# Negated softmax sum, division on GpSimd, and gated norms of two chunks in one

## The chip, the cores and the metric

The kernel runs on one core of one Trainium2 chip. Its time is the device time of one execution in microseconds (us); three runs of the kernel before took 1565.5, 1568.16 and 1681.18 us, and the median is 1568.16 us. Engines are called by the profile's names: PE is TensorE's matmuls and PEld its weight loads, DVE is VectorE, ACT is ScalarE, POOL is GpSimd, SP is SyncE, whose queue issues most DMAs.

## What is computed

One layer over 1024 latent tokens and 256 context tokens, width 1024. Half of the width goes through a gated DeltaNet (4 heads of 128, a forward and a backward scan, summed), half through neighbourhood attention (8 heads of 64, a window of keys and all context keys). Both go through one output projection; a SwiGLU network follows. The change touches two places: the attention's softmax and the norm that closes the DeltaNet.

```
S = S * exp(g_last) + k_dec^T v_new                    # scan step, carried state
o = rms_norm(o_f + o_b, out_norm_w) * silu(z)          # gated norm, per head
s = concatenate([q k_win + bias, q k_ctx])             # per query: 384 places of the window, 256 context keys
p = softmax(s)                                         # one softmax over both
```

## The kernel before, in words

The work comes in stages, in program order: modulation and input projections; tables for the scan; then a stage in which the two scans and the attention run beside each other; then the output projection (L1282, L1432) and the network (L1305, L1646). A scheduler lays out each engine's instructions near the order in which the program issues them; after that each engine's queue is in order.

*Scan.* Tokens are cut into ten chunks of 128, two of context (0, 1) and eight latent ones (2 to 9). `ORDER` gives each direction its order: forward 0 to 9, backward 1, 0, 9 down to 2. The loop at L1246 takes ten steps, called scan steps 0 to 9 here; each issues the loads for the next (`load`, six DMAs of 256 KB a chunk) and runs one chunk of each direction. `scan(d, c)` is a generator: keys times state (L1163, corrected at L1165), queries times state (L1173, into the sum `oacc` at L1176 or L1179), the triangular product (L1182, scaled at L1186 and L1188), the local product (L1194, added at L1195), and the state's update (L1199, L1205). A latent chunk is visited twice, once by each direction; from step 6 on both chunks of a step are visited for the second time, and `scan` goes on into `finish(c)`.

*Gated norm.* `finish` loads `z`, squares `oacc` on ACT with a sum for each head (L1220), computes the reciprocal root from an integer guess and three Newton steps on DVE (`rsqrt`, L179 to L184), scales by it and by `z` (L1227), and two turns later transposes the chunk on PE and splits it in two for the output projection (`turned`, L1109, L1112, L1113). It issues 14 small DVE instructions on 128x4 numbers. The two chunks that end last are turned only behind the first matmuls of the output projection.

*Attention beside the scan.* `attention` is a generator too. It goes through 32 pairs of halves; a half is 128 queries of one head against 640 scores. Each `next` of a scan or finish generator is a turn, and each turn adds `PACE` = 0.72 steps of attention (`beside`). `pair` computes a pair's scores into PSUM (L302), and for each half adds the bias and takes the maximum (L304, in place in the bias tile `bt`), negates the maximum (L306), takes the exponential with its sum (L307, ACT), the reciprocal (L308) and the product with it (L309). Two steps later come five transposes a half (L314), a copy out of PSUM (L317), and the values' products (L324). Bias tiles come by DMA (L271), their context part by a memset on GpSimd (L270), one pair ahead, in four buffers. GpSimd's only other work here is the split of finished attention output (L372), twice a pair of heads.

Of the kernel before, what the change touches and what calls it, by code (L numbers as in the profile page):

```python
# [9 lines left out]
F32 = mybir.dt.float32  # L10
# [3 lines left out]
AF = mybir.ActivationFunctionType  # L14
OP = mybir.AluOpType
# [44 lines left out]
def run(*gens):  # L60

    live = [g for g in gens if g is not None]
    while live:
        live = [g for g in live if next(g, 0) != 0]
# [24 lines left out]
def hybrid(ctx, tc, a, dbg):  # L89
# [20 lines left out]
    bias = lasting("bias", [128, 8])  # L110
# [142 lines left out]
    def attention(nw):  # L253

        def load(hd):
            qs = nw.tile([128, L], F16, name="qs", tag="qs", bufs=4)
            kh = nw.tile([128, T], F16, name="kh", tag="kh", bufs=4)
            kl = nw.tile([128, T], F16, name="kl", tag="kl", bufs=4)
            sp.dma_start(qs, nq_d[hd].rearrange("i d t -> (i d) t"))
            for i in range(2):  # L260
                sp.dma_start(kh[i * 64:i * 64 + 64], nk_d[0, hd])
                sp.dma_start(kl[i * 64:i * 64 + 64], nk_d[1, hd])
            return qs, kh, kl

        def biases(hp, half, cb):

            out = []
            for u, w0 in enumerate(WIN):
                bt = nw.tile([128, 640], F32, name="bt", tag="bt", bufs=4)
                pool.memset(bt[:, CTX[w0]], 0.0)  # L270
                sp.dma_start(bt[:, w0:w0 + 384], a["rpb"][2 * hp + u, half, CASE[cb]])  # L271
                out.append(bt)
            return out

        def values(hp, half, cb):
            vw = nw.tile([128, 3, 128], F32, name="vw", tag="vw", bufs=3)
            sp.dma_start(vw, vw_d[:, cb, half:half + 3, hp * 128:hp * 128 + 128])
            return vw

        def context(hp):  # L280
            vc = nw.tile([128, 2, 128], F32, name="vc", tag="vc")
            sp.dma_start(vc, nv_d[0:CT, hp * 128:hp * 128 + 128].rearrange("(c p) d -> p c d", p=128))
            return vc

        def pair(heads, bts, vw, vc, half, cb, out):

            r0 = 4 * half
            sc = psum[-1].tile([128, 1536], F32, name="sc", tag="sc", bufs=2)
            mx = nw.tile([128, 2, 4], F32, name="mx", tag="mx", bufs=3)
            for u, (head, w0, bt) in enumerate(zip(heads, WIN, bts)):  # L290
                qs, kh, kl = head
                q = qs[:, (half * 4 + cb) * 128:(half * 4 + cb + 1) * 128]
                kv = [kx[:, CT:].rearrange("p (r c) -> p r c", c=64)[:, r0:r0 + 12, BLKS[cb]:BLKS[cb] + 32]
                      for kx in (kh, kl)]
                parts = [(CTX[w0].start, CTX[w0].stop, (kh[:, 0:CT], kl[:, 0:CT]))]
                if w0:
                    parts += [(256, 512, [x[:, 0:8] for x in kv]), (512, 640, [x[:, 8:12] for x in kv])]
                else:
                    parts += [(0, 384, kv)]
                for n0, n1, ks in parts:  # L300
                    for i in range(2):
                        pe.matmul(sc[:, u * 640 + n0:u * 640 + n1], q, ks[i], start=i == 0, stop=i == 1)  # L302
                m = mx[:, u]
                dve.tensor_tensor_reduce(bt, sc[:, u * 640:u * 640 + 640], bt, 1.0, -3.0e38, OP.add, OP.max,  # L304
                                         m[:, 0:1])
                dve.tensor_scalar(m[:, 1:2], m[:, 0:1], -1.0, None, op0=OP.mult)  # L306
                act.activation(bt, bt, AF.Exp, bias=m[:, 1:2], accum_out=m[:, 2:3])  # L307
                dve.reciprocal(m[:, 3:4], m[:, 2:3])  # L308
                dve.tensor_scalar(bt, bt, m[:, 3:4], None, op0=OP.mult)  # L309
            yield 1  # L310
            pts = []
            for u, bt in enumerate(bts):
                for j in range(5):
                    pe.transpose(sc[:, u * 640 + j * 128:u * 640 + (j + 1) * 128],  # L314
                                 bt[:, j * 128:(j + 1) * 128], ident)
                pt = nw.tile([128, 640], F32, name="pt", tag="pt", bufs=3)
                act.copy(pt, sc[:, u * 640:u * 640 + 640])  # L317
                pts.append(pt)
            yield 1
            for j in range(5):  # L320
                for u, (w0, pt) in enumerate(zip(WIN, pts)):
                    vals = [vc[:, i] for i in range(2)] + [vw[:, i] for i in range(3)]
                    vv = (vals[j] if w0 else vals[(j + 2) % 5])[:, u * ND:u * ND + ND]
                    pe.matmul(sc[u * ND:u * ND + ND, 1280:1408], vv, pt[:, j * 128:(j + 1) * 128],  # L324
                              start=j == 0, stop=j == 4)
            act.copy(out.rearrange("p (r b c) -> p r b c", r=8, b=4)[:, :, cb],
                     sc[:, 1280:1408].rearrange("p (r c) -> p r c", r=8))
            yield 1

        order = [(hp, half, cb) for hp in range(NAH // 2) for half in range(2) for cb in range(4)]  # L330
        heads = {0: [load(0), load(1)]}
        vcs = {0: context(0)}
        bt, vw = biases(*order[0]), values(*order[0])
        yield 1
        old = None
        for n, (hp, half, cb) in enumerate(order):
            if half == 1 and cb in (0, 2) and hp + 1 < NAH // 2:
                heads.setdefault(hp + 1, []).append(load(2 * hp + 2 + cb // 2))
                if cb == 0:
                    vcs[hp + 1] = context(hp + 1)  # L340
            if cb == 0:
                out = nw.tile([128, 512], F32, name="no", tag="no")
            if old:
                next(old)
            cur = pair(heads[hp], bt, vw, vcs[hp], half, cb, out)
            next(cur)
            if n + 1 < len(order):
                bt, vw = biases(*order[n + 1]), values(*order[n + 1])
            yield 1
            if old:  # L350
                next(old)
                if cb == 0:
                    store(*done)
            if cb == 3:
                done = out, hp, half
            old = cur
            yield 1
        next(old)
        yield 1
        next(old)  # L360
        store(*done)
# [753 lines left out]
    with ExitStack() as gs:  # L1115
# [10 lines left out]
        def work(name, bufs=2, dt=F32):  # L1126
            return sw.tile([128, 4, 128], dt, name=name, tag=name, bufs=bufs)
# [25 lines left out]
        def scan(d, c):  # L1153
# [52 lines left out]
                                                 op0=OP.mult, op1=OP.add)  # L1206
                S[d] = sn
            yield 1
            if lat:
                if c in seen:  # L1210
                    yield from finish(c)
                seen.add(c)

        def finish(c):
            o = oacc[:, c - 2]
            z, sq = work("z"), work("sq", 1)
            sp.dma_start(fl(z), z_d[(c - 2) * 128:(c - 1) * 128])
            r = sw.tile([128, 4], F32, name="orr", tag="orr")
            for h in range(4):
                act.activation(sq[:, h], o[:, h], AF.Square, accum_out=r[:, h:h + 1])  # L1220
            t = sw.tile([128, 3, 4], F32, name="nwt", tag="nwt")
            dve.tensor_tensor(r, r, RQ2[:, c - 2], OP.mult)
            dve.tensor_scalar(t[:, 0], r, 1.0 / DH, EPS, op0=OP.mult, op1=OP.add)
            rsqrt(r, t[:, 0], t[:, 1])
            dve.tensor_tensor(r, r, RQ[:, c - 2], OP.mult)
            for h in range(4):
                dve.scalar_tensor_tensor(o[:, h], o[:, h], r[:, h:h + 1], z[:, h], op0=OP.mult, op1=OP.mult)  # L1227
            if c in last:
                return
            yield 1  # L1230
            yield 1
            turned(c)
            yield 1

        last = [ORDER[0][-1], ORDER[1][-1]]
        count = [0.0]

        def beside(n):
            count[0] += n
# [6 lines left out]
        for i in range(NCH):  # L1246
            if i + 1 < NCH:
                for d in range(2):
                    load(d, ORDER[d][i + 1])
            live = [scan(d, ORDER[d][i]) for d in range(2)]  # L1250
            while live:
                nxt = []
                for n, g in enumerate(live):
                    if next(g, 0):
                        nxt.append(g)
                    beside(PACE)
                live = nxt
        for _ in fill:
            pass

# [467 lines left out]
```

## Time and profile before

| What | Value |
|---|---|
| median of three runs | 1568.16 us |
| profiled execution | 1568.91 us, span 1566.9 us |
| busy in the span | PE 1480.1, PEld 1234.1, DVE 997.3, ACT 720.3, POOL 233.3 us |
| scan steps 2 to 5 | 619.7 to 710.4 us |
| scan steps 6 to 9 | 710.4 to 833.2 us |
| first matmul of the output projection | 833.27 us |

The page gives busy time, the span in 40 slices, the chain of work that ended last, and the costliest groups of instructions. A group's row has the line, engine and operation, output and inputs, shape and count, then busy time and mean time of one, then the engine's idle time ahead of it and what ended that. Stretches of the span can be asked for one by one; their rows give busy time and number of instructions of each engine, the granted clock as a share, the DMA engines' busy share and GB/s. Timeline rows begin with start and duration in us. Matmul records are pipelined and overlap, so a busy PE is not a full one.

### The profile page before, as it was taken

To read this page: it belongs to the slowest core of one execution; us is meant where nothing else is said; L and a number is where in the kernel's file an instruction comes from. 1 tells how busy PE (TensorE), PEld (TensorE's weight loads), DVE (VectorE), ACT (ScalarE), POOL (GpSimd) and SP (SyncE) were. 2 spreads that over 40 slices of the span, in tenths; PEclk is the share of its full clock that TensorE was granted. 3 is DMA by queue.
4 is the path that set the end of the run, shared out by engine and by line. 5 is a ranking of instruction groups with operands and counts; after the bars stand their busy time and mean duration, and the time that the engine had idled before them with its cause. 6 is when DMAs were issued, how large, how long until landed. Compare 5 with 4: busy or idle time off the path is not lost. (4 is left out here: it accounts for less than half of the span.)

```text
span 1566.9 us, 24037 instructions
## 1 busy us (share of the span) xinstructions
PE 1480.1 (94%) x8702; PEld 1234.1 (79%) x8702; DVE 997.3 (64%) x1856; ACT 720.3 (46%) x1378; POOL 233.3 (15%) x280
## 2 busy tenths in 40 slices
PE   6999999999988987998899999999999999999999
PEld 4788787678887766887688878888888888888887
DVE  5774596583253644678887559966556556689642
ACT  6443554653343544766664257333333334454440
POOL 1154401642343600111100000000000000000000
PEclk9999999999999998999999999999999999999999
DMA  9263222675455449899845710632233324698742
GB/s 389 64 214 125 72 75 68 197 240 187 132 158 187 163 130 301 261 285 291 251 135 185 259 47 23 231 124 101 102 107 107 102 101 143 225 379 287 242 149 81
DMA packets 206551, 271.04 MB, mean 173 GB/s; under 512 B 16096, under 2 KB 115936, under 8 KB 205408
## 3 DMA queue, kind: packets, MB, share of 16 engines
q1 hardware_dynamic: 200816, 264.73, 51.2%
q10 hardware_dynamic: 5616, 4.76, 0.9%
q8 instruction: 69, 1.13, 0.3%
q14 instruction: 50, 0.41, 0.1%
HBM read 204.69 MB, written 68.94 MB: 175 GB/s over the span
## 5 line engine op out<-in xcount | busy, mean ns | idle before, releaser
L403 PE MATMUL blk<-hh,whi 128*128 128x512 f32 (+1 forms) x410 | 122.8, 394 | 1.4 <-ACT kk L548 1.4
L1366 ACT CAST uhi<-wq 128x512 fp32r<-128x512 f32 x101 | 61.1, 622 | 134.1 <-issue 84.6
L1366 ACT CAST uhi<-ws 128x512 fp32r<-128x512 f32 x91 | 53.9, 621 | 146.5 <-PE ps L1305 92.4
L403 PE MATMUL blk<-hh,wlo 128*128 128x512 f32 (+1 forms) x410 | 116.9, 381 | 0.6 <-POOL wlo L200 0.6
L403 PE MATMUL blk<-hl,whi 128*128 128x512 f32 (+1 forms) x410 | 116.2, 379 | 0.3 <-DVE hl L689 0.3
L1367 DVE TENSOR_TENSOR ulo<-wq,uhi 128x512 fp32r<-128x512 f32 x101 | 67.9, 689 | 59.0 <-ACT uhi L1366 32.6
L1305 PE MATMUL ps<-hT,uhi 128*128 128x512 f32 x336 | 103.6, 390 | 0.0
L1305 PE MATMUL ps<-lT,uhi 128*128 128x512 f32 x336 | 103.5, 389 | 0.0
L1305 PE MATMUL ps<-hT,ulo 128*128 128x512 f32 x336 | 103.5, 389 | 0.0
L1305 PE MATMUL ps<-hB,uhi 128*128 128x512 f32 x288 | 89.2, 391 | 0.6 <-ACT hB L1480 0.6
L1305 PE MATMUL ps<-lB,uhi 128*128 128x512 f32 x288 | 88.8, 390 | 0.4 <-DVE lB L1481 0.4
L1305 PE MATMUL ps<-hB,ulo 128*128 128x512 f32 x288 | 88.7, 389 | 0.0
L586 PE MATMUL blk<-zhi,hh 128*128 128x256 f32 (+1 forms) x288 | 84.7, 294 | 0.7 <-ACT kk L548 0.7
L403 PEld LDWEIGHTS blk<-hh,wlo 128*128 128x128 f32 x410 | 72.9, 194 | 15.4 <-POOL wlo L200 0.9
L403 PEld LDWEIGHTS blk<-hl,whi 128*128 128x128 f32 x410 | 73.0, 194 | 14.6 <-DVE hl L689 0.6
L586 PE MATMUL blk<-zhi,hl 128*128 128x256 f32 (+1 forms) x288 | 83.1, 289 | 0.0
L403 PEld LDWEIGHTS blk<-hh,whi 128*128 128x128 f32 x410 | 70.0, 195 | 16.6 <-issue 4.0
L586 PE MATMUL blk<-zlo,hh 128*128 128x256 f32 (+1 forms) x288 | 81.8, 284 | 0.0
L1305 PEld LDWEIGHTS ps<-hT,ulo 128*128 128x128 f32 x336 | 63.1, 188 | 13.2
L1305 PEld LDWEIGHTS ps<-lT,uhi 128*128 128x128 f32 x336 | 63.1, 188 | 13.1
L1305 PEld LDWEIGHTS ps<-hT,uhi 128*128 128x128 f32 x336 | 63.0, 188 | 12.9
L200 POOL TENSOR_TENSOR wlo<-wraw,whi 128x1024 fp32r<-128x1024 f32 x18 | 44.2, 2455 | 176.6 <-ACT whi L199 163.2
(359 smaller groups left out, 3652.6 us busy)
## 6 DMA issues: line engine op xcount, KB each, us to landing
wq<-w_fo SPq DMA_DIRECT2D x99, 256.0 KB, 4.3
wq<-w_gu SPq DMA_DIRECT2D x88, 256.0 KB, 2.9
wad<-wa SPq DMA_DIRECT2D x64, 256.0 KB, 3.7
bt<-rpb SPq DMA_DIRECT2D x64, 192.0 KB, 4.0
t_d<-g SPq DMA_DIRECT2D x22, 512.0 KB, 3.9
fr<-t_d SPq DMA_DIRECT2D x44, 256.0 KB, 4.5
f_d<-g SPq DMA_DIRECT2D x33, 256.0 KB, 2.1
fr<-f_d SPq DMA_DIRECT2D x33, 256.0 KB, 3.7
```

Of the source, the lines that this page charges most:

```text
L200: lo_engine.tensor_tensor(o, r, h.bitcast(F32), OP.subtract)
L403: pe.matmul(o, ww[:, k], xx[k][:, s], start=k == 0 and j == 0, stop=k == KT - 1 and j == 2)
L586: pe.matmul(p[:, :c1 - c0], x[k][:, s], ww[:, k, c0:c1], start=k == 0 and j == 0, stop=k == KT - 1 and j == 2)
L1305: pe.matmul(o, w[wi][:, k], x[xi][:, k], start=first and k == 0 and j == 0, stop=k == n - 1 and j == 2, skip_group_check=True)
L1366: act.copy(hi, self.raw[key])
L1367: dve.tensor_tensor(lo, self.raw[key], hi.bitcast(F32), OP.subtract)
```

## The change

In the softmax L304 writes the negated sum of scores and bias and takes its minimum, which is the negated maximum of the sum. The exponential takes it as its bias, with a scale of -1, so the instruction at L306 goes. The product with the reciprocal moves from DVE to GpSimd.

```diff
-                dve.tensor_tensor_reduce(bt, sc[:, u * 640:u * 640 + 640], bt, 1.0, -3.0e38, OP.add, OP.max,
+                dve.tensor_tensor_reduce(bt, sc[:, u * 640:u * 640 + 640], bt, -1.0, 3.0e38, OP.add, OP.min,
                                          m[:, 0:1])
-                dve.tensor_scalar(m[:, 1:2], m[:, 0:1], -1.0, None, op0=OP.mult)
-                act.activation(bt, bt, AF.Exp, bias=m[:, 1:2], accum_out=m[:, 2:3])
+                act.activation(bt, bt, AF.Exp, scale=-1.0, bias=m[:, 0:1], accum_out=m[:, 2:3])
                 dve.reciprocal(m[:, 3:4], m[:, 2:3])
-                dve.tensor_scalar(bt, bt, m[:, 3:4], None, op0=OP.mult)
+                pool.tensor_scalar(bt, bt, m[:, 3:4], None, op0=OP.mult)
```

In the scan a chunk that has been visited twice is put on a list, `ended`. The next scan step takes the list's two chunks into one `finish` that runs as a third generator beside the two scans; the last two finish behind the loop, with no attention step added. One chain of small instructions, on 128x8 numbers, serves both chunks.

```diff
-            if lat:
-                if c in seen:
-                    yield from finish(c)
+            if c in seen:
+                ended.append(c)
+            elif lat:
                 seen.add(c)
 
-        def finish(c):
...
+        def finish(cs):
+            cs = sorted(cs)
+            two = slice(cs[0] - 2, cs[1] - 1, cs[1] - cs[0])
+            os, zs = [oacc[:, c - 2] for c in cs], [work("z") for c in cs]
+            r = sw.tile([128, 2, 4], F32, name="orr", tag="orr")
+            for i, c in enumerate(cs):
+                sp.dma_start(fl(zs[i]), z_d[(c - 2) * 128:(c - 1) * 128])
+                sq = work("sq", 1)
+                for h in range(4):
+                    act.activation(sq[:, h], os[i][:, h], AF.Square, accum_out=r[:, i, h:h + 1])
+            yield 1
+            t = sw.tile([128, 3, 2, 4], F32, name="nwt", tag="nwt")
+            dve.tensor_tensor(r, r, RQ2[:, two], OP.mult)
+            dve.tensor_scalar(t[:, 0], r, 1.0 / DH, EPS, op0=OP.mult, op1=OP.add)
             rsqrt(r, t[:, 0], t[:, 1])
+            dve.tensor_tensor(r, r, RQ[:, two], OP.mult)
+            for i, c in enumerate(cs):
+                for h in range(4):
+                    dve.scalar_tensor_tensor(os[i][:, h], os[i][:, h], r[:, i, h:h + 1], zs[i][:, h],
+                                             op0=OP.mult, op1=OP.mult)
+                yield 1
+            for c in cs:
+                if c not in last:
+                    yield 1
+                    turned(c)
...
-            live = [scan(d, ORDER[d][i]) for d in range(2)]
+            live = [scan(d, ORDER[d][i]) for d in range(2)] + [finish(ended)] * bool(ended)
+            ended = []
...
+        run(finish(ended))
         for _ in fill:
             pass
```

More of the change, by code (lines that the diff above doesn't have):

```diff
@@ L1208, in scan @@
             yield 1
-            if lat:
-                if c in seen:
-                    yield from finish(c)
+            if c in seen:
+                ended.append(c)
+            elif lat:
                 seen.add(c)
-        def finish(c):
[L1215 to L1222, printed above, removed]
+        def finish(cs):
[11 more added lines that the diff above has]
+            dve.tensor_tensor(r, r, RQ2[:, two], OP.mult)
@@ L1223, in finish @@
             dve.tensor_scalar(t[:, 0], r, 1.0 / DH, EPS, op0=OP.mult, op1=OP.add)
             rsqrt(r, t[:, 0], t[:, 1])
[L1225 to L1233, printed above, removed]
+            dve.tensor_tensor(r, r, RQ[:, two], OP.mult)
@@ L1235, in hybrid @@
+            for i, c in enumerate(cs):
[7 more added lines that the diff above has]
+                    turned(c)
         last = [ORDER[0][-1], ORDER[1][-1]]
-        count = [0.0]
+        count, ended = [0.0], []
         def beside(n):
```

## The prediction

> **What bounds the kernel now.** The page comes first, for the span and the chain of work that ended last. The profiled execution took 1568.91 us, 0.75 us over the median of 1568.16; the sum below is made against 1568.91.
>
> ```profile
> span 1566.9 us, 24037 instructions
> ```
>
> The chain of waits, from 938 us on, is little else than TensorE:
>
> ```profile
> 938.24 320.97 PE ps L1305 x1416
> ...
> 1353.60 209.45 PE ps L1646 x924
> ```
>
> All that the change touches lies before that and ends where the output projection starts, at 833 us. After it matmuls of L1282, L1305 and L1646 follow one another, so a shorter scan stage moves the end by as much. The next view is busy time by stretch. Its columns: length, busy time (and instructions) of PE, weight loads, DVE, ACT and POOL, granted clock, DMA share, GB/s.
>
> ```profile
> 619.70:710.40 90.70, 85.72 (x822) 75.42 (x820) 63.70 (x203) 58.88 (x152) 12.06 (x28) 1.00 0.94 277
> 710.40:833.20 122.80, 107.78 (x1004) 92.25 (x1002) 103.88 (x390) 78.44 (x210) 13.43 (x33) 0.97 0.67 204
> ```
>
> The first row holds scan steps 2 to 5, where no chunk is finished; the second holds steps 6 to 9, where each step finishes two. Matmul records overlap, so I read TensorE's fill from its weight loads, one for each matmul: 75.42/90.70 = 83% in the plain stretch, 92.25/122.80 = 75% in the other. VectorE does the reverse: 70% and 85%. Cut finer, at the first state read (L1163) of each step and at the end of its last state update:
>
> ```profile
> 710.40:733.40 23.00, 21.24 (x202) 18.70 (x201) 18.12 (x62) 15.12 (x47) 3.42 (x7) 1.00 0.93 288
> 733.40:745.70 12.30, 9.78 (x92) 7.29 (x91) 11.57 (x59) 8.00 (x17) 1.25 (x4) 1.00 1.01 300
> 745.70:768.90 23.20, 19.85 (x185) 17.56 (x186) 19.43 (x58) 15.41 (x47) 3.14 (x7) 1.00 0.90 274
> 768.90:782.60 13.70, 10.34 (x81) 8.18 (x77) 12.07 (x58) 7.86 (x16) 1.89 (x3) 0.75 0.70 211
> 782.60:805.50 22.90, 21.55 (x211) 19.51 (x211) 18.91 (x63) 16.27 (x48) 2.49 (x8) 1.00 0.49 154
> 805.50:816.40 10.90, 9.09 (x89) 6.94 (x86) 10.44 (x55) 7.13 (x15) 0.93 (x3) 1.00 0.41 128
> 816.40:833.20 16.80, 15.94 (x160) 14.07 (x158) 13.34 (x41) 8.65 (x23) 0.31 (x1) 1.00 0.10 32
> ```
>
> The short stretches are the finishing parts: 12.30 + 13.70 + 10.90 = 36.9 us in which no scan step runs, VectorE is 94%, 88% and 96% busy and weight loads 59 to 64%. There VectorE is the bound. Elsewhere TensorE is nearest to full and loses time to waits in its queue.
>
> **The change, part by part.** The rows that price it, VectorE groups from 710.4 to 833.2 us:
>
> ```profile
> L309 DVE TENSOR_SCALAR bt<-bt,mx 128x640 f32<-128x640 f32 x34 | 19.8, 585 | 0.2
> ...
> L1227 DVE SCALAR_TENSOR_TENSOR oacc<-oacc,orr,z 128x128 f32<-128x128 f32 x24 | 6.8, 346 | 0.3 <-DVE mx L308 0.3
> ...
> L306 DVE TENSOR_SCALAR mx<-mx 128x1 f32<-128x1 f32 x34 | 4.9, 146 | 0.1
> ...
> L184 DVE SCALAR_TENSOR_TENSOR orr<-nwt,orr 128x4 f32<-128x4 f32 x18 | 2.8, 156 | 0.0
> ...
> L180 DVE TENSOR_SCALAR orr<-nwt 128x4 int32<-128x4 int32 x6 | 1.0, 167 | 0.0
> ```
>
> *VectorE's load, steps 6 to 9.* The 34 divisions (19.8 us) leave for GpSimd and the 34 negations (4.9 us) go. A norm is 14 small instructions of 156 to 167 ns; six norms stand here (L180 x6), some 13.2 us. Two chunks at once make three of them, on 8 numbers instead of 4, which I price the same since 128x1 and 128x4 take 146 and 156: 6.6 us go. The eight L1227 of a pair of chunks remain. 103.9 - 19.8 - 4.9 - 6.6 = 72.6 us.
>
> *The finishing parts.* They now run beside the next scan step. The count of turns that feeds attention stays: 6 + 5x8 + 3x14 + 8 = 96 before, 6 + 6x8 + 3x14 = 96 after. So steps 6 to 9 hold the same TensorE work with VectorE no longer the bound, and I let them run at the fill of the plain stretch: 92.25/0.83 = 110.9 us, a gain of 11.9 us. VectorE would then be 72.6/110.9 = 65% busy, less than the plain stretch's 70%, so nothing contradicts that fill. What is late next is TensorE's own queue, as in steps 2 to 5. Bounds: no gain if the waits only change their names, 20 us at a fill of 90%.
>
> *VectorE's load, steps 2 to 5.* L309 and L306 there:
>
> ```profile
> 619.70:710.40 90.70, 13.17 (x24) 1.00 0.94 277
> ```
>
> ```profile
> 619.70:710.40 90.70, 3.39 (x24) 1.00 0.94 277
> ```
>
> 16.6 of 63.7 us leave an engine that was not the bound; TensorE misses 15.3 us there. I take 2 us for other VectorE steps that no longer queue behind a division; bounds 0 and 8.
>
> *The division on GpSimd.* The trace shows no GpSimd multiply by a column. Nearest rows:
>
> ```profile
> L372 POOL TENSOR_TENSOR na<-no,na 128x512 fp32r<-128x512 f32 x8 | 10.2, 1278 | 32.6 <-ACT na L371 32.6
> ...
> L197 POOL CAST whi<-fraw 128x1024 fp32r<-128x1024 f32 x1 | 1.2, 1236 | 13.2 <-DMA fraw<-w_conv 13.2
> ```
>
> By elements, 640 columns cost 0.77 us at the cast's rate (one stream in, one out) and 1.6 us at the two-input rate. I take 0.8, nearest in form to the cast. It stands between the reciprocal and the transposes, 0.25 us longer than the 0.55 of VectorE, plus a hop between engines. What the negation's removal gives back on the same chain:
>
> ```profile
> 710.87 0.08 DVE L304 DVE_READ_ACCUMULATOR2_ANT mx<- 128x1 f32 x1
> ...
> 710.98 0.15 DVE L306 TENSOR_SCALAR mx<-mx 128x1 f32<-128x1 f32 x1
> ...
> 711.22 0.83 ACT L307 ACTIVATE bt<-bt,mx 128x640 f32<-128x640 f32 x1 [0.38 <-DVE mx L306]
> ```
>
> From the minimum's readout (710.95) to the exponential is 0.27 us, of which the hop of 0.10 stays. So the chain changes by +0.25 + 0.10 - 0.17 = about +0.2 us for each half, or less where other VectorE work stood ahead of negation or division. I take 0, for TensorE rarely waited on the division:
>
> ```profile
>   PE sc L314: 0.9, 1
> ```
>
> That is the division's list of who waited for it: one wait of TensorE in 64. If every one of the 58 halves from 619.7 us on were exposed, +0.2 would cost 12 us. Queues: the next bias tables' memsets stand ahead of the divisions in GpSimd's order (those of pair n+1 before the divisions of pair n), so no table waits for a division; the eight L372 stand between and hold one 1.28 us at most. The Trainium skill ("GPSIMD Engine Reference", Engine selection) speaks against the move: elementwise work belongs on VectorE, GpSimd being about half as fast on two inputs and near line rate on one; its best loop of 1.8 cycles an element gives an estimate of 0.96 us here. No run shows it yet; by it the chain would be 0.16 us longer, at most 9 us over all halves, and the sum 1565.
>
> *A shared port.* GpSimd and VectorE hold each other up already:
>
> ```profile
> 747.11 1.27 POOL L372 TENSOR_TENSOR na<-no,na 128x512 fp32r<-128x512 f32 x1 [4.13 <-ACT na L371]
> 747.19 1.54 DVE L309 TENSOR_SCALAR bt<-bt,mx 128x640 f32<-128x640 f32 x1
> ```
>
> A division of 0.55 us lasted until GpSimd was done. In the last norm it meets instructions of 0.17 us:
>
> ```profile
> 834.18 1.27 DVE L180 TENSOR_SCALAR orr<-nwt 128x4 int32<-128x4 int32 x1
> ```
>
> So a norm's small instructions, with all operands in SBUF, can each be held by a running division, up to 0.8 us. Instructions with an operand in PSUM are not lengthened so; the softmax's first pass has 824 ns at the median and 826 at most:
>
> ```profile
> L304 DVE CUSTOM_DVE_ANT_0 bt<-sc,bt x64: 804/824/826, 588.6 to 823.6; 128x640 f32<-128x640 f32 x64
> ```
>
>  The Trainium skill ("Advanced Engine Details and Errata", VectorE Performance Modes) says that the second VectorE port is shared with GpSimd and the two block each other; the trace agrees with 1.54 us.
>
> *The moved DMAs.* The eight z loads keep count and size; two issue per finish, beside the next scan's loads on SP, and are needed only after the norm. Cost 0.
>
> *The tail.* The last two chunks finish after the last scan step, as before. Cover:
>
> ```profile
> 833.27 1.16 PE L1282 MATMUL ps<-na,whi 128*128 128x512 f32 x4 [0.88 <-DVE oacc L1195]
> ...
> 843.80 0.62 PE L1282 MATMUL ps<-na,wlo 128*128 128x512 f32 x2
> ```
>
> ```profile
> 839.61 0.15 DVE L182 TENSOR_TENSOR nwt<-orr 128x4 f32<-128x4 f32 x1
> ...
> 841.57 1.14 DVE L1227 SCALAR_TENSOR_TENSOR oacc<-oacc,orr,z 128x128 f32<-128x128 f32 x4
> ```
>
> Matmuls run 11 us; the chain ends now at 842.7. Ten small instructions take 1.96 us, so one norm of 14 takes 2.8, and the tail gets no longer: 0. But step 9 has 14 turns instead of 8, so attention ends after the scan and its last half is followed by little: +1 us (0 to 4).
>
> **Sum:** 1568.9 - 11.9 - 2 + 0 + 1 = 1556.0 us.
>
> **The rivals.** *DMA takes over.* From 710.4 to 782.6 us the queues are 70 to 101% busy and moved 288x23.0 + 300x12.3 + 274x23.2 + 211x13.7 = 19.6 MB; at 300 GB/s, the most in these rows, 65.2 of 72.2 us. The gain there would stop at 7 us; from 782.6 on it is 50.6 - 40.5/0.83 = 1.8 us; steps 2 to 5 (0.94) give nothing: 1568.9 - 8.8 = about 1560. Against it: TensorE's longest waits from 619.7 to 833.2 us are on engines, and no load is in that list.
>
> ```profile
> PE sc L314 <- ACT pt L317: 5.8, 7, 1.3
> PE sc L302 <- DVE mx L304: 3.4, 5, 1.6
> ```
>
>
> *The norm delays the scan (slower than before).* Its 14 small instructions (2.8 us) and eight gatings at 0.28 (2.3 us) now stand in VectorE's queue among the steps that carry the state. If the state waits for all of it in three steps, 15.3 us, plus one held instruction each (2.4 us): 1556.0 + 17.7 = about 1574. It decides from 4.3 us a step on (12.9/3). For it: the queue is in order. Against it: turns alternate, and 35% of VectorE's time would be free.
>
> *The transposes wait for GpSimd (slower).* At 1.6 us a division the chain is 1.05 + 0.10 - 0.17 = 0.98 us longer; with all 58 halves exposed 57 us, 1613. It eats the gain from 0.22 us a half on. Against it: the cast's row and the one wait of 0.9 us.
>
> *A larger gain.* At a fill of 92% in both stretches: 167.7/0.92 = 182.3 of 213.5 us, 31 us: 1538 and below.
>
> **How the numbers follow.** Forecast 0.52, around 1556 (1548 to 1563 for it alone); DMA 0.19; norm 0.16; transposes 0.06; larger gain 0.07. The range of 1541 (20 and 8 us gained) to 1574 leaves out most of the last two. About 2% (31 us) is what a measurement of this kernel can tell from no change: faster by over 2% 0.06, slower 0.05, within 0.89.
>
> **What would show it.** Right: VectorE below 70% from scan step 6 on, the weight loads' share there near 83%, no stretch without a scan step between steps, GpSimd's multiply near 0.8 us, the exponential 0.1 us behind the minimum's readout. Wrong: transposes whose wait ends on GpSimd, state updates (L1205) behind the norm, waits on loads, small norm instructions above 0.5 us, a division above 1.2 us.

## The result: slower, and the profile after

The changed kernel took 1599.24 us (median of four runs, 1591.89 to 1601.86), the kernel before 1572.31 us (four runs). The ratio is 1.0168, 95% interval 1.0138 to 1.0197; it leaves out the run of 1681.18 us, which lies 7% above the other three. The forecast was 1556.0, with a range of 1541 to 1574: the result lies beyond its upper end, on the other side of no change. The profiled execution took 1591.89 us.

In the changed kernel lines stand one or more lower: exponential L306, reciprocal L307, division L308, transposes L313, copy out L316, gating by `z` L1231. Its page, where the division is now the first of the costliest groups:

```profile
span 1589.8 us, 23869 instructions
...
L308 POOL TENSOR_SCALAR bt<-bt,mx 128x640 f32<-128x640 f32 x64 | 120.9, 1898 | 96.6 <-DVE mx L307 80.6
...
L313 PE MATMUL sc<-cst,bt 128*128 128x128 f32 x320 | 53.1, 296 | 40.6 <-POOL bt L308 38.6
```

One division takes 1.90 us; the forecast took 0.8, with 0.77 and 1.6 as bounds. TensorE idled 40.6 us before the transposes, of which 38.6 ended with the division. Busy time by stretch, steps 2 to 5 and steps 6 to 9, with the columns of the rows shown before:

```profile
620.70:730.60 109.90, 91.98 (x827) 79.19 (x825) 51.02 (x157) 60.29 (x153) 57.10 (x54) 0.95 0.77 227
730.60:855.20 124.60, 105.36 (x1004) 90.49 (x1002) 87.97 (x280) 79.35 (x213) 78.01 (x68) 1.00 0.68 203
```

Steps 2 to 5 went from 90.7 to 109.9 us, steps 6 to 9 from 122.8 to 124.6. Their start moved by 1.0 us (619.7 to 620.7), and the rest behind them grew by 0.9 (1566.9 - 833.2 = 733.7; 1589.8 - 855.2 = 734.6). So nearly all of the net loss lies in steps 2 to 5, where the forecast expected 2 us of gain. In steps 6 to 9 what the other two parts of the change gain covers most of the loss: against the same kernel with its division on VectorE, shown below, the two stretches are 17.2 and 7.3 us longer.

Part of the 19.2 us in steps 2 to 5 is TensorE's granted clock, 0.95 in the row above and 1.00 in the same stretch before. It is low in one place, and TensorE's longest wait for a division lies there too:

```profile
630.00:640.00 10.00, 6.38 (x27) 5.25 (x27) 3.47 (x11) 5.65 (x15) 6.18 (x5) 0.61 0.16 45
```

```profile
633.17 1.33 PE L313 MATMUL sc<-cst,bt 128*128 128x128 f32 x5 [3.08 <-POOL bt L308]
```

The clock accounts for at most 5% of 109.9, or 5.5 us (an estimate from the two rows). In steps 6 to 9 it is the kernel before that has the lower clock, 0.97 against 1.00, at most 3.7 us by the same estimate. Whether a wait brings the low clock about is not shown.

VectorE fell to 46% and 71% busy, as intended; the weight loads, the measure of TensorE's fill, fell with it, to 72% and 73%. The division's own list, durations (least, median, most) and who waited for it:

```profile
L308 POOL TENSOR_SCALAR bt<-bt,mx x64: 1881/1888/2234, 588.9 to 850.0; 128x640 f32<-128x640 f32 x64
...
  PEld sc L313: 50.5, 51
  PE sc L313: 38.6, 44
```

Where TensorE's matmuls waited for a division once before, they wait 44 times, and the weight loads 51 times. The timeline of two halves shows it:

```profile
737.32 1.89 POOL L308 TENSOR_SCALAR bt<-bt,mx 128x640 f32<-128x640 f32 x1
737.47 0.08 DVE L304 DVE_READ_ACCUMULATOR2_ANT mx<- 128x1 f32 x1
737.59 0.83 ACT L306 ACTIVATE bt<-bt,mx 128x640 f32<-128x640 f32 x1 [0.76 <-DVE mx L304]
...
739.26 0.53 PEld L313 LDWEIGHTS sc<-cst,bt 128*128 128x128 f32 x5 [0.88 <-POOL bt L308]
739.26 0.77 PE L313 MATMUL sc<-cst,bt 128*128 128x128 f32 x5 [0.69 <-POOL bt L308]
739.43 1.89 POOL L308 TENSOR_SCALAR bt<-bt,mx 128x640 f32<-128x640 f32 x1
```

The division ends at 739.21, and the weights of its transposes load from 739.26, after 0.88 us of idling. The other end of the chain did what was forecast: the exponential starts 0.04 us behind the minimum's readout (737.55, 737.59).

### The profile page after: what moved, and what is told of

Same layout as the page of the kernel before. It is cut to its first block, busy times and chain, and to the rows that moved or that the text cites. A ratio compares the mean times of both kernels' runs of the same rounds, so it can differ in the third digit from the quotient of the medians.

```text
span 1589.8 us, 23869 instructions
## 1 busy us (share of the span) xinstructions
PE 1481.9 (93%) x8702; PEld 1235.2 (78%) x8702; DVE 961.8 (61%) x1672; ACT 721.5 (45%) x1378; POOL 349.1 (22%) x344
## 5 line engine op out<-in xcount | busy, mean ns | idle before, releaser
L308 POOL TENSOR_SCALAR bt<-bt,mx 128x640 f32<-128x640 f32 x64 | 120.9, 1898 | 96.6 <-DVE mx L307 80.6
L313 PE MATMUL sc<-cst,bt 128*128 128x128 f32 x320 | 53.1, 296 | 40.6 <-POOL bt L308 38.6
L1311 PE MATMUL ps<-hB,ulo 128*128 128x512 f32 x288 | 88.7, 389 | 0.0
L304 DVE CUSTOM_DVE_ANT_0 bt<-sc,bt 128x640 f32<-128x640 f32 x64 | 52.5, 821 | 51.7 <-issue 22.8
```

Of the source, the lines that this page charges most:

```text
L308: pool.tensor_scalar(bt, bt, m[:, 3:4], None, op0=OP.mult)
L1311: pe.matmul(o, w[wi][:, k], x[xi][:, k], start=first and k == 0 and j == 0, stop=k == n - 1 and j == 2, skip_group_check=True)
```

## The experiments

The main theory: the division on GpSimd is over three times as long as on VectorE and TensorE's transposes stand bare behind it. Rivals: the merged norm delays the scan; GpSimd and VectorE hold each other up; bias tables come late behind the divisions; VectorE's load never was what the finishing parts paid for. The table has the medians, the ratio to the kernel before (measured beside it on the same chip) with its 95% interval, and scan steps 2 to 5 and 6 to 9 in the profiled execution, from the first matmul of keys times state of a step to that of another, or of the output projection. The medians and ratios rest on all of a kernel's runs, the two stretches on one execution each; the granted clock in a stretch is 0.95 to 1.00.

| Kernel | median us | ratio [95%] | steps 2-5 | steps 6-9 |
|---|---|---|---|---|
| before | 1572.31 | 1 | 90.7 | 122.8 |
| after | 1599.24 | 1.0168 [1.0138, 1.0197] | 109.9 | 124.6 |
| division on VectorE | 1564.20 | 0.9944 [0.9924, 0.9963] | 92.7 | 117.3 |
| division alone | 1603.93 | 1.0184 [1.0158, 1.0210] | 107.1 | 134.2 |
| merged norms alone | 1570.68 | 0.9987 [0.9969, 1.0005] | 91.5 | 122.0 |
| negated sum alone | 1567.33 | 0.9969 [0.9949, 0.9988] | 92.9 | 120.2 |
| no division | 1554.61 | 0.9890 [0.9875, 0.9906] | 92.7 | 108.0 |
| GpSimd's product aside | 1562.62 | 0.9953 [0.9935, 0.9971] | 95.5 | 112.9 |
| scores first | 1581.72 | 1.0063 [1.0044, 1.0082] | 103.3 | 118.6 |
| two-input division | 1572.36 | 1.0003 [0.9989, 1.0017] | 98.4 | 118.8 |
| split by halves | 1567.84 | 0.9982 [0.9963, 1.0002] | 98.1 | 115.0 |
| two-input, scores first | 1569.50 | 0.9992 [0.9974, 1.0011] | 98.5 | 115.8 |
| VectorE's product aside | 1563.23 | 0.9951 [0.9930, 0.9973] | 92.1 | 117.5 |

### One part of the change at a time

*Division back on VectorE*, in the changed kernel:

```diff
-                pool.tensor_scalar(bt, bt, m[:, 3:4], None, op0=OP.mult)
+                dve.tensor_scalar(bt, bt, m[:, 3:4], None, op0=OP.mult)
```

> The changed kernel with the division put back on VectorE (negated sum and merged norms stay). If the late transposes behind a 1.89 us GpSimd multiply are the cause, the loss goes: faster than the kernel before, 1550 to 1566 us, the multiply at about 0.55 us and no transpose waiting on GpSimd. If the merged norms delay the scan, it stays slow, 1585 us or more. If both matter alike, about 1575 us.

1564.20 us, ratio 0.9944: the loss is gone, and what is left of the change is a small gain. Its two stretches:

```profile
620.20:712.90 92.70, 87.02 (x822) 75.95 (x820) 62.12 (x178) 58.60 (x152) 12.31 (x28) 1.00 0.94 272
712.90:830.20 117.30, 107.95 (x1005) 91.99 (x1003) 99.91 (x314) 78.46 (x213) 15.68 (x34) 0.99 0.72 213
```

*Division alone*, in the kernel before:

```diff
-                dve.tensor_scalar(bt, bt, m[:, 3:4], None, op0=OP.mult)
+                pool.tensor_scalar(bt, bt, m[:, 3:4], None, op0=OP.mult)
```

> The kernel before with the division alone moved to GpSimd (negation and norms as before). If the division is the cause: slower than the changed kernel, since here neither the negation's removal nor the merged norms give anything back: 1600 to 1625 us, transposes waiting some 80 us on GpSimd. If the norms are the cause: within 5 us of the kernel before.

1603.93 us, ratio 1.0184: this one line carries the whole loss, and the other two parts give back little of it. So the merged norm is not what made the kernel slower. Of this kernel's profiled loss 6.6 us lie before step 2 (626.3 against 619.7).

*Merged norms alone*: the kernel before with the change's `ended`, `finish(cs)` and the third generator, and its old softmax.

```diff
-            live = [scan(d, ORDER[d][i]) for d in range(2)]
+            live = [scan(d, ORDER[d][i]) for d in range(2)] + [finish(ended)] * bool(ended)
+            ended = []
```

> The kernel before with the merged norms alone (division and negation on VectorE). If the division is the cause of the loss: 4 to 12 us faster than before, the stretch from scan step 6 on shorter. If the norms delay the scan: 10 us slower or more, state updates behind the norm's small instructions.

1570.68 us, ratio 0.9987 with 1 in its interval: no gain that can be measured, and no loss. The 4 to 12 us of gain that were expected did not come. In steps 6 to 9 VectorE is still 100.81/122.0 = 83% busy:

```profile
713.20:835.20 122.00, 108.02 (x1006) 91.46 (x1003) 100.81 (x348) 79.24 (x215) 15.00 (x34) 0.99 0.72 206
```

*Negated sum alone*: the kernel before with the change's L304 and exponential.

```diff
-                dve.tensor_scalar(m[:, 1:2], m[:, 0:1], -1.0, None, op0=OP.mult)
-                act.activation(bt, bt, AF.Exp, bias=m[:, 1:2], accum_out=m[:, 2:3])
+                act.activation(bt, bt, AF.Exp, scale=-1.0, bias=m[:, 0:1], accum_out=m[:, 2:3])
```

> The kernel before with the negated sum alone. By both theories 0 to 6 us faster, the exponential 0.1 us behind the minimum's readout. A loss here would speak against both.

1567.33 us, ratio 0.9969: a gain of some 5 us. With the norms' 0.9987 it makes 0.9956, within the interval of the two together (0.9944).

### Is it the load, the wait or the port?

*No division*: L308 left out of the changed kernel.

```diff
-                pool.tensor_scalar(bt, bt, m[:, 3:4], None, op0=OP.mult)
```

> The changed kernel without any division (the probabilities stay undivided). It shows the most that taking the division off VectorE can give. By the forecast's steps (VectorE no longer the bound from scan step 6 on, a shorter chain) 1545 to 1558 us. If VectorE's load never set the pace, about the 1564 us of the kernel with the division on VectorE.

1554.61 us, ratio 0.9890:

```profile
617.10:709.80 92.70, 88.65 (x826) 76.53 (x825) 51.33 (x157) 58.57 (x153) 11.53 (x29) 1.00 0.94 272
709.80:817.80 108.00, 104.23 (x1004) 90.35 (x1002) 84.33 (x280) 78.87 (x213) 14.34 (x34) 1.00 0.78 236
```

Steps 6 to 9 take 108.0 us where the forecast had 110.9, at a fill of 90.35/108.0 = 84% where it had 83%. Had the division cost nothing, the sum would have come out: 1556.0 forecast, 1554.61 measured. In part that is luck: steps 2 to 5 took 4.0 us more than forecast (92.7 against 88.7), steps 6 to 9 2.9 less, and step 2 began 2.6 us earlier (617.1 against 619.7).

*GpSimd's product aside*: the changed kernel with the 64 products on a half-precision tile that nothing reads. The pool of that tile, and the smaller tile for the norm's squares that makes room for it, are not printed here.

```diff
-                pool.tensor_scalar(bt, bt, m[:, 3:4], None, op0=OP.mult)
+                aside = side[0].tile([128, 640], F16, name="aside", tag="aside")
+                pool.tensor_scalar(aside, bt, m[:, 3:4], None, op0=OP.mult)
```

> The changed kernel, but GpSimd's multiply writes a tile that nobody reads, so the transposes take the undivided table (the division is left out of the result; the squares' unused output is one head wide to make room). GpSimd does the same 64 multiplies of about 1.9 us. If only the wait of the transposes costs: within 4 us of the kernel without division. If GpSimd's work itself costs, by the port it shares with VectorE or by memsets queued behind it: 1585 us or more.

1562.62 us, ratio 0.9953, with the same 1.89 us on GpSimd. That lies between the two times that were expected (within 4 us of the kernel without division, or 1585 and more). Both stretches take 95.5 + 112.9 = 208.4 us, against 234.5 in the changed kernel and 200.7 without division. So of the 33.8 us that GpSimd's division costs over none at all, 26.1 go when the transposes no longer wait for it. The ratios give the same share: 1.0168 - 0.9953 = 0.0215 of 1.0168 - 0.9890 = 0.0278. The other 7.7 stay with GpSimd's product here, and the list of waits shows some of their causes: what ended VectorE's waits before the softmax's first pass, and SP's before the bias tables' loads, from 619.8 to 828.2 us:

```profile
DVE bt L304 <- POOL bt L270: 8.6, 8, 2.7
DVE bt L304 <- DMA bt<-rpb: 7.2, 5, 2.7
```

```profile
SPq L271 <- POOL aside L309: 21.2, 19, 1.8
```

Those two waits make 15.8 us; without division they make 3.2 + 2.6 = 5.8. The tables' buffers come free late, because here the product aside must have read them too. In the changed kernel these two waits make 5.0 + 0.6 us: there the transposes come behind the division and are what frees the buffers. So how much GpSimd's load by itself costs the changed kernel is not shown.

*VectorE's product aside*: the same with the product on VectorE, so that its load stays and the chain to the transposes is without it.

```diff
-                pool.tensor_scalar(aside, bt, m[:, 3:4], None, op0=OP.mult)
+                dve.tensor_scalar(aside, bt, m[:, 3:4], None, op0=OP.mult)
```

> The changed kernel with its 64 divisions on VectorE, written to a half-precision tile of their own that nothing reads; the transposes take the undivided exponentials, so the probabilities are left undivided, and the squares of the norm go to one tile a head wide for room. VectorE keeps the 35 us of load, the chain to the transposes is without its 0.55 us. It stands between the kernel without any division (1554.6 us, steps 6 to 9 in 108.0 us) and the one with the division on VectorE (1564.2, 117.3). Theory A, the forecast's: VectorE's load is what steps 6 to 9 pay for: the time stays near 1562 to 1566 and these steps near 117. Theory B, the length of the chain in front of the transposes is what they pay for, here as in the changed kernel: 1555 to 1558, steps 6 to 9 near 109.

1563.23 us, ratio 0.9951:

```profile
617.80:709.90 92.10, 87.29 (x822) 75.88 (x820) 63.11 (x180) 58.28 (x152) 11.77 (x28) 1.00 0.92 270
709.90:827.40 117.50, 107.60 (x1004) 92.00 (x1002) 98.20 (x314) 81.15 (x218) 14.39 (x34) 0.99 0.75 217
```

117.5 us, beside 117.3 with the division in the chain and 108.0 without its load. A chain shorter by 0.55 us gives nothing here; VectorE's load is what steps 6 to 9 pay for. Nor do late tables explain it: VectorE's first passes wait 4.1 us for them here, and 5.8 without division. The clock, 0.99 here and 1.00 without division, is at most 1.2 of the 9.5 us (an estimate). That VectorE's load is paid for was the forecast's theory, and it holds. In steps 2 to 5 all three take 92 to 93: neither matters there.

### How far the wait depends on the division's length

*Scores first*: in the changed kernel a pair's scores are issued ahead of the previous pair's transposes.

```diff
-            if old:
-                next(old)
             cur = pair(heads[hp], bt, vw, vcs[hp], half, cb, out)
             next(cur)
+            if old:
+                next(old)
```

> The changed kernel with a pair's scores issued ahead of the previous pair's transposes, which gives the multiply some 1.1 us of TensorE work more to hide behind. If the wait of the transposes is the cost: 12 to 22 us faster than the changed kernel, 1575 to 1587 us. If GpSimd's work itself costs: no faster than 1594 us.

1581.72 us, ratio 1.0063: about 1% comes back. The list of who waited for the division falls from 50.5 and 38.6 us to

```profile
  PEld sc L313: 39.7, 38
  PE sc L313: 30.5, 33
```

The profiled execution (1587.41 us, 6 above its median) reaches step 2 only at 629.9 us; the later kernel with the same order reaches it at 620.1, so this isn't put down to the order.

*Two-input division*: the product written with two tensor inputs, the second the column repeated.

```diff
-                pool.tensor_scalar(bt, bt, m[:, 3:4], None, op0=OP.mult)
+                pool.tensor_tensor(bt, bt, m[:, 3:4].to_broadcast([128, 640]), OP.mult)
```

> The changed kernel with the division as a GpSimd tensor-tensor multiply, the column spread over 640 elements. At the two-input rate of the kernel before (1278 ns for 512) it should take about 1.6 us instead of 1.89. If the cost goes with the multiply's length: 0.29 us less for each of 64 halves, nearly all exposed, some 15 us faster than the changed kernel, 1580 to 1588 us. If not: unchanged at 1595 to 1602 us.

```profile
L308 POOL TENSOR_TENSOR bt<-bt,mx 128x640 f32<-128x640 f32 x64 | 79.8, 1256 | 110.1 <-DVE mx L307 80.4 <-DMA kl<-nk_d 12.2 <-DMA y<-y_d 5.1
```

1572.36 us, ratio 1.0003. The expected 1.6 us and 1580 to 1588 were both missed: the form with more inputs is the shorter, 1.26 us instead of 1.90. That the cost goes with the product's length holds. For 58 halves 0.64 us less takes 234.5 - 217.2 = 17.3 us off the two stretches, 0.30 a half, of which up to 3.5 us may be the clock (0.95 and 0.98 in steps 2 to 5; an estimate). The medians differ by more, 26.9 us, since the profiled execution of the changed kernel is the fastest of its four.

*Forms on GpSimd by themselves*: behind the scan stage, in the kernel before, four times each on a tile of their own.

```diff
+        for _ in range(4):
+            pool.tensor_scalar(t0, t0, col, None, op0=OP.mult)
+            pool.tensor_scalar(t0[:, :320], t0[:, :320], col, None, op0=OP.mult)
+            pool.tensor_scalar(t0[:, :128], t0[:, :128], col, None, op0=OP.mult)
+            pool.tensor_scalar(t0, t0, 1.0, None, op0=OP.mult)
+            pool.tensor_tensor(t0, t0, col.to_broadcast([128, 640]), OP.mult)
+            pool.tensor_tensor(t0, t0, t1, OP.mult)
+            pool.tensor_copy(t1, t0)
```

> The kernel before, with trial instructions on GpSimd behind the scan stage, where GpSimd has little else to do: each form four times on a tile of its own, whose result nothing reads. In the changed kernel one multiply of 128x640 by a column took 1.89 us (TENSOR_SCALAR), and 1.26 us when written with two tensor inputs, the second a column repeated. Theory A, the column as a scalar operand is dear for each element: the multiply by a constant takes 0.8 to 1.3 us, by the column 1.9; 320 and 128 columns take about 0.95 and 0.4. Theory B, TENSOR_SCALAR is slow on GpSimd whatever its scalar: the multiply by a constant takes 1.9 too. Theory C, a fixed start of about a microsecond for the column: 640, 320 and 128 columns take 1.9, 1.4 to 1.5 and 1.1 to 1.2. The two-input forms 1.26 (repeated column) and, by the 1278 ns of the 512 columns of the attention's split, 1.6 (dense); the copy 0.8. The time of the kernel stays within 0.3% of before.

The timeline of the third repeat:

```profile
1024.45 2.72 POOL L1562 TENSOR_SCALAR trial<-trial,ones 128x640 f32<-128x640 f32 x1
1027.27 2.11 POOL L1563 TENSOR_SCALAR trial<-trial,ones 128x320 f32<-128x320 f32 x1
1029.47 0.96 POOL L1564 TENSOR_SCALAR trial<-trial,ones 128x128 f32<-128x128 f32 x1
1030.52 1.89 POOL L1565 TENSOR_SCALAR trial<-trial 128x640 f32<-128x640 f32 x1
1032.49 1.25 POOL L1566 TENSOR_TENSOR trial<-trial,ones 128x640 f32<-128x640 f32 x1
1033.82 1.90 POOL L1567 TENSOR_TENSOR trial<-trial 128x640 f32<-128x640 f32 x1
1035.78 1.06 POOL L1568 COPY trial<-trial 128x640 f32<-128x640 f32 x1
```

A product with a constant (L1565) takes 1.81 to 1.89 us in all four repeats, as long as one with a column in the softmax. That speaks for theory B, TENSOR_SCALAR is slow on GpSimd whatever its scalar. But the trial's own products with a column (L1562) took 2.20 to 2.72 us behind the first, so here the column was 0.3 to 0.9 us dearer than the constant; why it is dearer here than in the softmax is open. Two inputs take 1.25 to 1.70 with a repeated column (the 1.25 shown is the shortest of four) and 1.57 to 1.91 dense; a copy takes 1.06. The columns of 320 and 128 scatter too much (1.13 to 2.11, 0.96 to 1.49) to part a start from a rate, and the very first product took 10.45 us; both are left open. So is the kernel's time in its one run, 1584.43 us, more than was expected of it.

*Split by halves*: the changed kernel with the first half's division on GpSimd in the two-input form and the second's on VectorE.

```diff
-                pool.tensor_scalar(bt, bt, m[:, 3:4], None, op0=OP.mult)
+                if u == 0:
+                    pool.tensor_tensor(bt, bt, m[:, 3:4].to_broadcast([128, 640]), OP.mult)
+                else:
+                    dve.tensor_scalar(bt, bt, m[:, 3:4], None, op0=OP.mult)
```

> The changed kernel with the division of each pair's first half on GpSimd, in the two-input form of 1.26 us, and that of the second half on VectorE. Theory, that the transposes lie right behind the division and its length is what costs: the first half's division has the second half's softmax after it, before both are transposed, so only half of the divisions lie bare, and these at VectorE's price; VectorE is spared 10 of its 20 us in scan steps 6 to 9. Steps 6 to 9 then take 112 to 116 us and the kernel 1558 to 1563, a little below the 1564.2 of the changed kernel with all divisions on VectorE. Rival, that every division on GpSimd lies bare whichever half it is of: half of the 10 us by which all divisions in this form lie above those on VectorE (1572.4 against 1564.2), so about 1568.

1567.84 us, ratio 0.9982: the rival's 1568, and not the 1558 to 1563 of the theory. The profiled execution is the longest of its twelve, 1576.01 us. Its list of who waited for the first half's division:

```profile
  PEld sc L316: 19.6, 24
  PE sc L316: 12.8, 19
```

24 of 32 still wait. The first half's transposes stand ahead of the second's in TensorE's queue and need only their own half, so by the program's order the second half's softmax is no cover for the first half's division.

*Two-input form with scores first*: both edits in one.

> The changed kernel with the division in the two-input form (1.26 us) and a pair's scores issued ahead of the previous pair's transposes, so that TensorE has six more matmuls between the softmax and the transposes that wait for it. With the one-input form this order gave back 17.5 us of the changed kernel's time (1599.2 to 1581.7). If the waiting transposes are the cost, the order gives back most of what is left of it here: from 1572.4 to 1562 to 1566, and the transposes' waits on the division fall from 41 us to below 20. Rival, that the later start of attention (9 us lost before scan step 2 with this order) outweighs it: 1572 to 1580.

1569.50 us, ratio 0.9992. The waits on the division fell from 24.4 + 16.8 = 41.2 us (weight loads and matmuls) to 19.5 + 12.8 = 32.3, and not below the 20 that was expected; the time hardly fell: 1562 to 1566 was missed. Where the rest went is open. Among the kernels that divide, the changed one with its division on VectorE has the lowest time; it is 0.6% faster than the kernel before (0.9944, interval 0.9924 to 0.9963).

## Why the prediction was wrong, step by step

The forecast's sum and the profiled execution differ by 1591.9 - 1556.0 = 35.9 us: 109.9 - 88.7 = 21.2 in steps 2 to 5, 124.6 - 110.9 = 13.7 in steps 6 to 9, 1.0 before them, nothing behind. The median lies another 7.4 us higher, which no trace here divides up. That the time would stay within 2% of before (0.89) came true, but on the other side and through another mechanism.

- *The division on GpSimd* is the step that failed: its price, and the zero that it was given in the chain to the transposes. The forecast took 0.8 us, from the row of another operation; TENSOR_SCALAR takes 1.89, above the upper bound of 1.6. The bounds scaled by the count of inputs, and the runs show the operation's form to matter more: 1.85 (product with a constant), 1.06 (copy), 1.26 (two inputs, one repeated). The Trainium skill ("GPSIMD Engine Reference", Engine selection) was right that elementwise work belongs on VectorE: 1.89 against 0.58 us. Its figure of about line rate for one input, and the 0.96 us estimated from its best loop, are not borne out for this product; only the copy, at 1.06 us, comes near.
- *"I take 0, for TensorE rarely waited on the division."* This read the absence of a wait as slack. The timeline of the kernel before has the slack, and it is small:

```profile
650.41 0.55 DVE L309 TENSOR_SCALAR bt<-bt,mx 128x640 f32<-128x640 f32 x1
...
651.11 0.74 PE L314 MATMUL sc<-cst,bt 128*128 128x128 f32 x5
651.73 0.55 DVE L309 TENSOR_SCALAR bt<-bt,mx 128x640 f32<-128x640 f32 x1
652.69 0.77 PE L314 MATMUL sc<-cst,bt 128*128 128x128 f32 x5 [0.84 <-ACT pt L317]
```

  In this pair, from the division's end to the transposes it is 651.11 - 650.96 = 0.15 us and 652.69 - 652.28 = 0.41. What a longer division costs is seen between the two forms on GpSimd, whose load is there in both: 0.64 us more costs 0.30 us a half in the two stretches, nearly half of what is added. Whether zero would have held at 0.8 us is not shown. The line through the two forms puts 0.80 us at 204.9 us for both stretches, 4.2 above the 200.7 without division; that is an estimate from single executions.
- *The transposes wait for GpSimd* was the rival that came true, with a chance of 0.06. Its price was too low (1.6 us for 1.89) and its exposure too high: not 57 us with all halves exposed in full, but 33.8 us over no division at all, of which 26.1 go with the wait.
- *The finishing parts* were right in mechanism, shown by three kernels that differ in little but the division: 117.3 us with VectorE's load and chain, 117.5 with its load alone, 108.0 with neither. The 11.9 us forecast need the division's load to be gone at no price: 14.8 then. The norms and the negation alone give 5.5, from 122.8 to 117.3. Up to 3.7 us of either gain may be the clock, 0.97 in this stretch before (an estimate).
- *VectorE's load*, 72.6 us forecast in steps 6 to 9, was 88.0, and 84.3 without division. The subtraction mixed two measures. The groups of that stretch add to 124.8 us in the kernel before, while its busy time is 103.9: neighbouring records overlap, and a group that goes takes less than its own sum from the busy time. Without division the groups add to 94.8, 30.0 less, where the forecast took off 31.3; the busy time fell by 19.6. The 65% was 71%, or 78% without the waits; the fill was reached all the same.
- *Steps 2 to 5*: the 2 us did not come. Without any division they take 92.7 us, 2.0 more than before; VectorE's load is not paid for there.
- *A shared port.* The small norm instructions were held, as expected, but seldom. The integer guess, three times in steps 6 to 9, after and then without division:

```profile
L179 DVE TENSOR_SCALAR nwt<-nwt 128x8 int32<-128x8 int32 x3 | 1.1, 353 | 0.1
```

```profile
L179 DVE TENSOR_SCALAR nwt<-nwt 128x8 int32<-128x8 int32 x3 | 0.5, 172 | 0.1
```

  All small instructions of the three norms make 9.9 and 7.1 us: 2.8 us held in all, off the path.
- *No table waits for a division* nearly held in the changed kernel: its first passes wait 5.6 us for tables in the two stretches, 8.8 before, and twice in all for a division (2.1 us). With the product aside they did wait, since there the buffer's last reader is the division.
- *The rivals*: a norm that delays the scan is excluded (norms alone 0.9987), and DMA as the bound too (its share is 0.78 in the fastest steps 6 to 9, those without division). *The tail*: the rest behind the scan grew by 0.9 us, near the 1 us of the forecast, but also of the spread between kernels (733.7 to 734.8).

## What to carry to other kernels

Price a moved instruction by a row of its own operation on the new engine, and where there is none, let the upper bound be far above the rows that are there and take the exposure at that bound. That nobody waits for an instruction is no slack: measure from its end to its consumer's start in the timeline. Take busy time away in one measure only, the groups' sums or the stretch's busy time, for records overlap.

## What the runs showed of the hardware that was not expected

On GpSimd a product of 128x640 numbers with one scalar for each partition takes 1.89 us, and the same product written with two tensor inputs, one of them the column repeated, 1.26 us in the softmax (1.25 to 1.70 in the trial). With a constant in place of the column it takes about as long (1.81 to 1.89), though in the same trial the column took 2.20 to 2.72. A dense second input takes 1.57 to 1.91, and a plain copy 1.06. VectorE's first pass of the softmax, whose input lies in PSUM, kept its 821 ns beside the divisions on GpSimd.
